# Hybrid encoder trunk on one core: splitting the weights by transfers instead of by VectorE and GpSimd

## The chip, the core and the metric

One of the eight cores of one Trainium2 chip runs the whole program. The metric is the device time of one execution in microseconds. The kernel before took 1604.42 us, the median of three runs (1602.0 to 1606.68).

## The reference

The program computes two residual layers on 512 tokens of width 1024, in float32: a bidirectional Mamba-2 mixer in layer 0, a two-sided Hyena operator in layer 1, and after each of them a SwiGLU channel mixer and a gated input embedding. Cut to what matters:

```python
for i in range(2):
    hn = rms_norm(h, norm_mix[i])
    h = h + (mamba2_mixer if i == 0 else hyena_mixer)(hn, ...)
    h = h + swiglu(rms_norm(h, norm_ffn[i]), w1[i], w3[i], w2[i])   # (silu(h@w1) * (h@w3)) @ w2
    gate = sigmoid(rms_norm(h, norm_ple[i]) @ ple_gate[i])
    h = h + gate * (p[i] @ ple_proj[i])
return rms_norm(h, final_norm)
```

All time goes into products with weights, 1984 weight tiles of 128 x 128 in all.

## The kernel before

Every product of an activation `x` with a weight `w` is made from three TensorE products in a rounded 32-bit format: each operand is split into a high part (the value rounded to that format) and a low part (value minus high part), and `mm3` (lines 292 to 294) adds `w_hi x_hi`, `w_hi x_lo` and `w_lo x_hi` in PSUM. Activations lie as 128 x 512 tiles, so one weight tile costs three matmuls of 512 columns. Only the gate branch of the Mamba stage (`mix_z`, lines 677 to 679) turns the operands round and uses 256 columns.

The host packs the weight tiles in the order of use, eight to a block: `W` has 248 blocks of 128 x 1024 values, 512 KB each. `weight(key)` hands out the next tile; when the first tile of block b is asked for, `emit_block` has been called for all blocks up to b + 2 (`LOOKAHEAD`). `emit_block` (line 268) loads the block into `w_raw` from SyncE's queue, ScalarE rounds it into `w_hi` (line 274), and VectorE writes `w_lo = w_raw - w_hi` (line 275). For every other block of the Mamba input weights and of the Hyena input weights (`pool_lo`) GpSimd does the subtraction instead. `w_raw`, `w_hi` and `w_lo` have three buffers each; the last four blocks keep their parts in a pool of their own with four.

Blocks 2 to 49 are the Mamba input weights, eight groups of six blocks; 142 to 165 the Hyena input weights. The others are the two SwiGLU stages (66 blocks each), the output projections, gates and the projections of `p` (blocks 0 and 1, and 140 and 141).

`load_split` (line 375) does the same splitting for the constant matrices of the Hyena Fourier transforms: CH (filters, during the first SwiGLU), CF and CI (at the Hyena entry), five pieces of up to 512 KB, loaded from ScalarE's queue into the same `w_raw` buffers.

In a group of the Mamba stage, beside the weights: VectorE makes the five-tap convolution (`pre`, line 595), the decay matrices `M` (758, 759), `xw` (708), `y` (771, 780 and others); ScalarE copies PSUM results, among them the two that start the states `ST` (728, 730), and takes exponentials of `FB` (756); SyncE loads `FB` (750, one broadcast row to 128 partitions, four buffers); GpSimd masks `FB` (752), carries states (724) and makes `y` of line 740. TensorE's small products of a group are lines 688 to 719 (transposes, states) and 769 and 775 (outputs). PSUM has four tiles for weight products (`mm_ps`) and four for the rest (`aux_ps`).

Nothing orders the engines by hand: the framework sorts each engine's instructions at build time, roughly as they are written and as operands come ready, and each engine then runs its own list strictly in order. A DMA stands in the list of the engine whose queue issues it, and waits there.

Of the kernel before, what the change touches and what calls it, by code (L numbers as in the profile page):

```python
# [10 lines left out]
F32 = mybir.dt.float32  # L11
F32R = mybir.dt.float32r
AF = mybir.ActivationFunctionType
ALU = mybir.AluOpType

P = 128
T = 512
D = 1024
KD = D // P
# [3 lines left out]
NG = 8  # L23
NC = 4
TPB = 8
# [3 lines left out]
HALVED = 4  # L29
# [49 lines left out]
def hy_cols(q):  # L79
    return [16 + 2 * q, 8 + 2 * q, 17 + 2 * q, 9 + 2 * q, 2 * q, 2 * q + 1]  # L80
# [13 lines left out]
def weight_order():  # L94
    o = order_mk("proj_0", range(KD), range(2))
    for g in range(NG):
        o += order_ssd_in(g)
    o += order_mk("ssd_out", range(KD), range(0, 8))
    o += order_mk("ssd_out", range(KD), range(8, 16), hold=2)
    for i in range(2):  # L100
        for kind, j in ffn_seq():
            o += order_ffn_up(i, j) if kind == "up" else order_ffn_down(i, j)
        o += order_gate(i)
        if i == 0:
            o += order_mk("proj_1", range(KD), range(2))
            for q in range(KD // 2):
                o += order_mk("hy_in", hy_cols(q), range(KD))
            o += order_mk("hy_out", range(KD), range(0, 4))
            o += order_mk("hy_out", range(KD), range(4, 8), hold=2)
    return o  # L110
# [105 lines left out]
def body(ctx, tc, d, out_):  # L216
    nc = tc.nc
    V, A, G, PE = nc.vector, nc.scalar, nc.gpsimd, nc.tensor
# [1 line left out]
    const = ctx.enter_context(tc.tile_pool(name="const", bufs=1))  # L220
    hpool = ctx.enter_context(tc.tile_pool(name="hpool", bufs=1))
    apool = ctx.enter_context(tc.tile_pool(name="apool", bufs=32))
    wpool = ctx.enter_context(tc.tile_pool(name="wpool", bufs=3))
    npool = ctx.enter_context(tc.tile_pool(name="npool", bufs=1))
    dram = ctx.enter_context(tc.tile_pool(name="dram", bufs=1, space=bass.MemoryType.DRAM))
    psum = ctx.enter_context(tc.tile_pool(name="psum", bufs=4, space=bass.MemoryType.PSUM))
# [28 lines left out]

    order = weight_order()
    nblk = (len(order) + TPB - 1) // TPB
    blocks = {}
    kept = {}
    pos = [0]  # L260
    ssd_blocks = range(2, 2 + 6 * NG, 2)
    hy_first = order.index(("hy_in", 0, hy_cols(0)[0])) // TPB
    hy_blocks = range(hy_first + 2, hy_first + 3 * KD, 2)

    def pool_lo(b):
        return b in ssd_blocks or b in hy_blocks

    def emit_block(b):
        raw = wpool.tile([P, TPB, P], F32, tag="raw", name="w_raw", bufs=3)
        nc.sync.dma_start(raw, d["W"][b])  # L270
        pool = kept.get(b, wpool)
        hi = pool.tile([P, TPB, P], F32R, tag="hi", name="w_hi")
        lo = pool.tile([P, TPB, P], F32R, tag="lo", name="w_lo")
        A.copy(hi, raw)  # L274
        (G if pool_lo(b) else V).tensor_sub(lo, raw, hi.bitcast(F32))  # L275
        blocks[b] = (hi, lo)

    def weight(key, n=1):
        t = pos[0]
        assert order[t] == key, (order[t], key)  # L280
        pos[0] += n
        b = t // TPB
        for ahead in range(b, min(b + 1 + LOOKAHEAD, nblk)):
            if ahead not in blocks:
                emit_block(ahead)
        hi, lo = blocks[b]
        i = t % TPB
        return hi[:, i:i + n, :].rearrange("p a b -> p (a b)"), lo[:, i:i + n, :].rearrange("p a b -> p (a b)")
# [84 lines left out]
    def load_split(pool, src, tag):  # L373
        n = src.shape[1]
        hi = pool.tile([P, n], F32R, tag=tag + "h", name=tag + "h", bufs=1)
        lo = pool.tile([P, n], F32R, tag=tag + "l", name=tag + "l", bufs=1)
        for i in range(0, n, TPB * P):
            s = slice(i, min(n, i + TPB * P))
            raw = wpool.tile([P, TPB * P], F32, tag="raw", name="craw", bufs=3)[:, :s.stop - i]
            nc.scalar.dma_start(raw, src[:, s])  # L380
            A.copy(hi[:, s], raw)
            V.tensor_sub(lo[:, s], raw, hi[:, s].bitcast(F32))
        return hi, lo

    def forward_h(C, mv, U, pool):
# [74 lines left out]
    def hyena_filters(pool):  # L460
# [14 lines left out]
        A.copy(w3h, w3)  # L475
        V.tensor_sub(w3l, w3, w3h.bitcast(F32))
        CH = load_split(pool, d["CH"], "CH")
        yield

# [70 lines left out]
    def ssd(next_norm):  # L550
        pool = sctx.enter_context(tc.tile_pool(name="ssd", bufs=1))
        tags = ("pre", ("FB", "FB"), 4, 2)
        rt = npool.tile([P, NC], F32, tag="rt", name="rt", bufs=2)
        A.activation(rt[:, 0:1], eps_t, AF.Sqrt)
        emit_block(0)
        pr = ple_in(pool, 0, tags)
        nm = Norm("nmix0")
        for k in range(KD):
            nc.sync.dma_start(h[k], d["xT"][k])
        emit_block(1)  # L560
        nc.sync.dma_start(par, d["par"])
        o, n = PAR["cw"][0], PAR["cw"][1] + PAR["cb"][1]
# [422 lines left out]
    def hyena(nm, next_norm):  # L985
# [102 lines left out]
        for q in range(4):  # L1088
            project_u(2 * q)
            project_u(2 * q + 1)  # L1090
            project_x0(2 * q)
            if q == 0:
                CF = load_split(pool, d["CF"], "CF")
                CI = load_split(pool, d["CI"], "CI")
                cih, cil = (c.rearrange("p (fch par cs t) -> p fch par cs t", fch=2, par=2, cs=2) for c in CI)
            UH = convolve(q)
            if q:
                back(q - 1, pq.pop(q - 1))
            pq[q] = convolve_rest(*UH)
            project_x0(2 * q + 1)  # L1100
# [36 lines left out]
```

## Time and profile before

| | us |
|---|---|
| median of three runs | 1604.42 |
| profiled execution | 1609.28 |
| its span, first to last instruction | 1607.5 |
| TensorE busy (7698 matmuls) | 1561.5 |
| VectorE busy | 1057.8 |
| ScalarE busy | 673.7 |
| GpSimd busy | 206.8 |

The stages, in us from the start of the span: the projection of `p` and the first norm up to 45, the Mamba groups to 454, its output projection to 520, SwiGLU to 912, gate, projection and norm to 960, Hyena entry to 990, Hyena to 1198, SwiGLU to 1560, the last gate and norm to the end. Busy times of an engine can be set against the length of a stage; an engine that is busy all the time sets the length. The busy time of a TensorE row includes its pipeline, so a matmul of 512 columns that reads 390 ns is followed by the next after 226 ns.

### The profile page before, as it was taken

Reading aid. Unit: us, or ns where it says so; the run is one execution under the profiler, and the core shown is the slowest. Engines: PE = TensorE matmul, PEld = TensorE weight load, DVE = VectorE, ACT = ScalarE, POOL = GpSimd, SP = SyncE. Lnnn points to the kernel's source line nnn. Section 1 sums busy time; section 2 is a strip of 40 time slices with the busy share of each in tenths; the row PEclk is TensorE's granted clock in tenths of the full one; section 3 lists DMA queues with packets and bytes.
Section 4 is the critical chain, followed back from the end, with each engine's and each line's share of the span. In section 5 each row is a group of like instructions: output and inputs, shape, how many; then the busy total and the mean of one; then the engine's idle time right before and its main releaser. Section 6 shows DMA issues by size and latency. Waiting matters only on the chain.

```text
span 1607.5 us, 19878 instructions
## 1 busy us (share of the span) xinstructions
PE 1561.5 (97%) x7698; PEld 1300.9 (81%) x7698; DVE 1057.8 (66%) x1463; ACT 673.7 (42%) x1111; POOL 206.8 (13%) x153
## 2 busy tenths in 40 slices
PE   7999899999999999999999999999999999999998
PEld 5888778877788788888888877888888888888887
DVE  6778787888956686464345578899974434444464
ACT  6574565656434332232233444343253222222355
POOL 1254343443100000000000002232000000000000
PEclk9999999999999999999999999999999999999999
DMA  6343233433143333342332344333132323322332
GB/s 241 110 147 112 92 104 107 131 105 105 62 138 98 105 118 131 108 148 92 95 102 92 100 156 157 105 105 105 53 92 92 104 93 94 103 92 96 120 100 78
DMA packets 56005, 176.52 MB, mean 110 GB/s; under 512 B 5959, under 2 KB 7175, under 8 KB 54760
## 3 DMA queue, kind: packets, MB, share of 16 engines
q1 hardware_dynamic: 46864, 151.17, 29.5%
q10 hardware_dynamic: 9048, 24.10, 4.2%
q8 instruction: 60, 0.98, 0.2%
q14 instruction: 33, 0.27, 0.1%
HBM read 164.63 MB, written 10.62 MB: 109 GB/s over the span
## 4 chain that ended last, share of the span: by engine, by line
PE 76%; DVE 14%; DMA 4%; ACT 3%; issue 2%; POOL 1%; SPq 0%; ACTq 0%; POOLq 0%; DVEq 0%
PE mm_ps L294 22%; PE mm_ps L292 22%; PE mm_ps L293 22%; DMA FB<-FRd 2%; DVE w_lo L275 2%; DVE xw L708 1%; PE aux_ps L292 1%; PE aux_ps L293 1%; DVE pre L595 1%; PE aux_ps L294 1%; DVE M L758 1%; PE mm_ps L677 1%; PE mm_ps L679 1%; PE mm_ps L678 1%; DVE act L321 1%
## 5 line engine op out<-in xcount | busy, mean ns | idle before, releaser
L292 PE MATMUL mm_ps<-act,w_hi 128*128 128x512 f32 (+1 forms) x1856 | 723.3, 390 | 0.0
L293 PE MATMUL mm_ps<-act,w_hi 128*128 128x512 f32 (+1 forms) x1856 | 722.1, 389 | 0.9 <-DVE act L321 0.9
L294 PE MATMUL mm_ps<-act,w_lo 128*128 128x512 f32 (+1 forms) x1856 | 721.4, 389 | 0.2 <-DVE w_lo L275 0.2
L274 ACT CAST w_hi<-w_raw 128x1024 fp32r<-128x1024 f32 x248 | 259.8, 1050 | 598.2 <-PE mm_ps L293 435.5
L292 PEld LDWEIGHTS mm_ps<-act,w_hi 128*128 128x128 f32 x1856 | 349.4, 188 | 75.0 <-issue 5.1
L293 PEld LDWEIGHTS mm_ps<-act,w_hi 128*128 128x128 f32 x1856 | 349.3, 188 | 74.8 <-issue 3.6
L294 PEld LDWEIGHTS mm_ps<-act,w_lo 128*128 128x128 f32 x1856 | 349.3, 188 | 72.1 <-issue 2.7
L275 DVE TENSOR_TENSOR w_lo<-w_raw,w_hi 128x1024 fp32r<-128x1024 f32 x213 | 267.4, 1256 | 130.6 <-ACT w_hi L274 118.5
L275 POOL TENSOR_TENSOR w_lo<-w_raw,w_hi 128x1024 fp32r<-128x1024 f32 x35 | 98.9, 2825 | 726.6 <-ACT w_hi L274 704.9
L867 DVE TENSOR_TENSOR fb<-mm_ps,R 128x512 f32<-128x512 f32 x44 | 30.4, 691 | 128.4 <-PE mm_ps L294 128.4
L595 DVE SCALAR_TENSOR_TENSOR pre<-mm_ps,par,pre 128x511 f32<-128x511 f32 (+1 forms) x128 | 93.1, 739 | 3.3 <-ACT pre L591 3.2
L756 ACT ACTIVATE FB<-FB,bcol 128x128 f32<-128x128 f32 x256 | 79.6, 390 | 28.9 <-POOL FB L752 28.8
L864 DVE TENSOR_TENSOR fa<-mm_ps,R 128x512 f32<-128x512 f32 x44 | 30.3, 689 | 82.5 <-PE mm_ps L294 82.5
L875 DVE TENSOR_TENSOR h<-h,mm_ps 128x512 f32<-128x512 f32 x48 | 32.9, 686 | 72.4 <-PE mm_ps L294 72.4
L677 PE MATMUL mm_ps<-w_hi,act 128*128 128x256 f32 x256 | 72.6, 284 | 0.1
L678 PE MATMUL mm_ps<-w_lo,act 128*128 128x256 f32 x256 | 72.6, 284 | 0.0
L679 PE MATMUL mm_ps<-w_hi,act 128*128 128x256 f32 x256 | 72.4, 283 | 0.0
L752 POOL TENSOR_SCALAR_AFFINE_SELECT FB<-FB 128x512 f32<-128x512 f32 x64 | 54.5, 876 | 65.4 <-DMA FB<-FRd 57.4
L677 PEld LDWEIGHTS mm_ps<-w_hi,act 128*128 128x128 f32 x256 | 49.1, 192 | 0.5 <-issue 0.2
L678 PEld LDWEIGHTS mm_ps<-w_lo,act 128*128 128x128 f32 x256 | 49.1, 192 | 0.3
L679 PEld LDWEIGHTS mm_ps<-w_hi,act 128*128 128x128 f32 x256 | 49.1, 192 | 0.0
L320 ACT CAST act<-fb 128x512 fp32r<-128x512 f32 x44 | 27.4, 622 | 32.0 <-DVE fb L868 32.0
(264 smaller groups left out, 1610.1 us busy)
## 6 DMA issues: line engine op xcount, KB each, us to landing
w_raw<-W SPq DMA_DIRECT2D x248, 512.0 KB, 3.5
FB<-FRd SPq DMA_DIRECT2D x32, 512.0 KB, 5.4
pjd<-ppo ACTq DMA_DIRECT2D x16, 256.0 KB, 3.2
Hd<-Ht ACTq DMA_DIRECT2D x4, 1024.0 KB, 4.0
Ht<-Hd ACTq DMA_DIRECT2D x4, 1024.0 KB, 4.7
pj<-pjd ACTq DMA_DIRECT2D x12, 256.0 KB, 3.8
h<-xT SPq DMA_DIRECT2D x8, 256.0 KB, 5.9
dec<-dec ACTq DMA_DIRECT2D x4, 512.0 KB, 3.5
```

Of the source, the lines that this page charges most:

```text
L274: A.copy(hi, raw)
L275: (G if pool_lo(b) else V).tensor_sub(lo, raw, hi.bitcast(F32))
L292: PE.matmul(ps, whi, xhi, start=start, stop=False)
L293: PE.matmul(ps, whi, xlo, start=False, stop=False)
L294: PE.matmul(ps, wlo, xhi, start=False, stop=stop)
L595: V.scalar_tensor_tensor(pre[:, a:b], ps[:, a + o:b + o], pc("cw", 5 * c + j), pre[:, a:b], ALU.mult, ALU.add)
L677: PE.matmul(o, xhi[:, cs], whi, start=k == 0 and c % 2 == 0, stop=False)
L678: PE.matmul(o, xhi[:, cs], wlo, start=False, stop=False)
L679: PE.matmul(o, xlo[:, cs], whi, start=False, stop=k == KD - 1 and c % 2 == 1)
L752: G.affine_select(FB[:, dr], FB[:, dr], pattern=[[0, NC], [1 - 2 * dr, P]], compare_op=ALU.is_ge, fill=BIG, base=0, channel_multiplier=2 * ...
L756: A.activation(e, e, AF.Exp, bias=bcol[:, c, dr * 32 + hd:dr * 32 + hd + 1])
L875: V.tensor_add(h[m], h[m], ps)
```

## The change

The raw tiles are gone. The high part comes from a transfer that casts on its way from memory, issued by GpSimd (`emit_hi`). ScalarE writes the negative of the high part into the low part's tile, and a second transfer, also issued by GpSimd, adds the weights to it on its way (`accum_op=ALU.add`), which leaves weight minus high part. This holds for all 248 blocks and for the five pieces of the constant matrices. `emit_block(b)` also starts the casting load of block b + 1. High parts have five buffers, low parts four. Line numbers behind this place shift by 0 or 1.

```diff
-    wpool = ctx.enter_context(tc.tile_pool(name="wpool", bufs=3))
+    wpool = ctx.enter_context(tc.tile_pool(name="wpool", bufs=4))
...
-    blocks = {}
+    blocks, his = {}, {}
...
-    def pool_lo(b):
-        return b in ssd_blocks or b in hy_blocks
+
+    def emit_hi(b):
+        hi = kept.get(b, wpool).tile([P, TPB, P], F32R, tag="hi", name="w_hi", bufs=HALVED if b in kept else 5)
+        G.dma_start(hi, d["W"][b])
+        his[b] = hi
 
     def emit_block(b):
-        raw = wpool.tile([P, TPB, P], F32, tag="raw", name="w_raw", bufs=3)
-        nc.sync.dma_start(raw, d["W"][b])
-        pool = kept.get(b, wpool)
-        hi = pool.tile([P, TPB, P], F32R, tag="hi", name="w_hi")
-        lo = pool.tile([P, TPB, P], F32R, tag="lo", name="w_lo")
-        A.copy(hi, raw)
-        (G if pool_lo(b) else V).tensor_sub(lo, raw, hi.bitcast(F32))
+
+        if b not in his:
+            emit_hi(b)
+        hi = his.pop(b)
+        lo = kept.get(b, wpool).tile([P, TPB, P], F32R, tag="lo", name="w_lo", bufs=HALVED if b in kept else 4)
+        A.mul(lo, hi.bitcast(F32), -1.0)
+        G.dma_start(lo, d["W"][b], accum_op=ALU.add)
         blocks[b] = (hi, lo)
+        if 0 < b < nblk - 1:
+            emit_hi(b + 1)
...
-            raw = wpool.tile([P, TPB * P], F32, tag="raw", name="craw", bufs=3)[:, :s.stop - i]
-            nc.scalar.dma_start(raw, src[:, s])
-            A.copy(hi[:, s], raw)
-            V.tensor_sub(lo[:, s], raw, hi[:, s].bitcast(F32))
+            G.dma_start(hi[:, s], src[:, s])
+            A.mul(lo[:, s], hi[:, s].bitcast(F32), -1.0)
+            G.dma_start(lo[:, s], src[:, s], accum_op=ALU.add)
```

The lists of the engines change with it. The first matmuls on TensorE, before (`pp` is the split `p`, block 0 its weights, `S` and `dg` belong to the first norm):

```order
L292 MATMUL mm_ps<-pp,w_hi 128x512 x3
L293 MATMUL mm_ps<-pp,w_hi 128x512
L294 MATMUL mm_ps<-pp,w_lo 128x512
L292 MATMUL mm_ps<-pp,w_hi 128x512
L293 MATMUL mm_ps<-pp,w_hi 128x512
L294 MATMUL mm_ps<-pp,w_lo 128x512
```

And of the changed kernel:

```order
L293 MATMUL mm_ps<-pp,w_hi 128x512
L294 MATMUL mm_ps<-pp,w_hi 128x512
L348 MATMUL aux_ps<-ones,S 128x1 x4
L356 MATMUL aux_ps<-dg,ones 128x512
L295 MATMUL mm_ps<-pp,w_lo 128x512
L293 MATMUL mm_ps<-pp,w_hi 128x512
L294 MATMUL mm_ps<-pp,w_hi 128x512
L295 MATMUL mm_ps<-pp,w_lo 128x512 x2
```

The piece of the changed list begins with the last of four such pairs: eight products with the high part stand first, then both steps of the norm, and the first product with a low part comes after them.

VectorE in a Mamba group, around the `y` of line 771, before:

```order
L275 TENSOR_TENSOR w_lo<-w_raw,w_hi 128x1024
L598 SCALAR_TENSOR_TENSOR sx_1806<-sx_1806,pre 128x512
L799 TENSOR_SCALAR y<-y,rs 128x256 x6
L275 TENSOR_TENSOR w_lo<-w_raw,w_hi 128x1024
L595 SCALAR_TENSOR_TENSOR pre<-mm_ps,par,pre 128x510
L771 TENSOR_TENSOR y<-y,aux_ps 128x512
```

The same place in the changed kernel:

```order
L799 TENSOR_SCALAR y<-y,rs 128x256 x4
L598 SCALAR_TENSOR_TENSOR sx_1782<-sx_1782,pre 128x512
L799 TENSOR_SCALAR y<-y,rs 128x256
L595 SCALAR_TENSOR_TENSOR pre<-mm_ps,par,pre 128x510
L771 TENSOR_TENSOR y<-y,aux_ps 128x512
```

The two weight rows ahead of `y` are gone; the rest of the work keeps its order nearly.

GpSimd in one Mamba group, before:

```order
L740 TENSOR_TENSOR y<-XT,par 128x1024
L275 TENSOR_TENSOR w_lo<-w_raw,w_hi 128x1024
L752 AFFINE_SELECT FB<-FB 128x512 x2
L724 TENSOR_TENSOR stt<-ST,eL 128x256 x4
L752 AFFINE_SELECT FB<-FB 128x512 x2
L275 TENSOR_TENSOR w_lo<-w_raw,w_hi 128x1024
L752 AFFINE_SELECT FB<-FB 128x512 x4
L275 TENSOR_TENSOR w_lo<-w_raw,w_hi 128x1024
```

The first part of such a group in the changed kernel:

```order
L752 AFFINE_SELECT FB<-FB 128x512
L724 TENSOR_TENSOR stt<-ST,eL 128x256 x2
L752 AFFINE_SELECT FB<-FB 128x512
L274 DMA w_lo<-W 128x1024
L724 TENSOR_TENSOR stt<-ST,eL 128x256
L264 DMA w_hi<-W 128x1024
L752 AFFINE_SELECT FB<-FB 128x512 x3
L274 DMA w_lo<-W 128x1024
L264 DMA w_hi<-W 128x1024
L752 AFFINE_SELECT FB<-FB 128x512 x2
L274 DMA w_lo<-W 128x1024
```

Three subtractions of a group have become twelve DMAs, some of them behind masks that wait for `FB`; SyncE's list keeps only `FB` and the first and last transfers.

## Rows read from the trace of the kernel before

**Rows 1.** Busy us (and instructions) per engine in stages, then clock, DMA share, GB/s.
```profile
core 0: us, PE busy (x) PEld busy (x) DVE busy (x) ACT busy (x) POOL busy (x), PEclk, DMA share, GB/s
45.00:454.00 409.00, 388.13 (x2224) 326.91 (x2224) 333.82 (x483) 241.93 (x540) 153.01 (x126) 0.99 0.34 108
990.00:1198.00 208.00, 200.27 (x1026) 170.35 (x1025) 185.72 (x264) 77.69 (x107) 39.40 (x16) 0.99 0.30 97
1198.00:1560.00 362.00, 362.00 (x1600) 299.35 (x1599) 168.06 (x200) 111.86 (x134) 0.00 (x0) 1.00 0.31 100
```
**Rows 2.** TensorE's waits from 45 to 454 us: total us, times, longest.
```profile
PE aux_ps L775 <- DVE y L771: 8.6, 5, 3.3
PE aux_ps L719 <- DVE xw L708: 7.4, 6, 1.9
PE aux_ps L719 <- ACT w_hi L274: 3.6, 4, 1.1
```
**Rows 3.** Timeline in a Mamba group: start, duration, instruction [idle before it].
```profile
167.78 2.49 DVE L275 TENSOR_TENSOR w_lo<-w_raw,w_hi 128x1024 fp32r<-128x1024 f32 x1 [3.65 <-issue]
170.19 0.73 DVE L595 SCALAR_TENSOR_TENSOR pre<-mm_ps,par,pre 128x510 f32<-128x510 f32 x1
...
171.57 1.46 PE L775 MATMUL aux_ps<-ST,sC 128*128 128x512 f32 x2 [3.33 <-DVE y L771]
```
**Rows 4.** TensorE's waits from 945 to 1198 us, and VectorE's weight rows from 960.
```profile
PE aux_ps L1041 <- DVE act L1017: 5.5, 4, 1.9
...
L275 DVE TENSOR_TENSOR w_lo<-w_raw,w_hi 128x1024 fp32r<-128x1024 f32 x23 | 28.0, 1218 | 5.6 <-ACT w_hi L274 5.5
```
**Rows 5.** Groups by line, whole span: busy us, mean ns, idle before and releaser.
```profile
L275 DVE TENSOR_TENSOR w_lo<-w_raw,w_hi 128x1024 fp32r<-128x1024 f32 x213 | 267.4, 1256 | 130.6 <-ACT w_hi L274 118.5
...
L274 ACT CAST w_hi<-w_raw 128x1024 fp32r<-128x1024 f32 x248 | 259.8, 1050 | 598.2 <-PE mm_ps L293 435.5
```
**Rows 6.** Timeline of TensorE at the start.
```profile
10.46 0.63 PE L292 MATMUL mm_ps<-pp,w_hi 128*128 128x512 f32 x1
...
10.89 0.63 PE L293 MATMUL mm_ps<-pp,w_hi 128*128 128x512 f32 x1
...
18.34 1.02 PE L355 MATMUL aux_ps<-dg,ones 128*128 128x512 f32 x2
...
21.96 0.39 PE L294 MATMUL mm_ps<-pp,w_lo 128*128 128x512 f32 x1
...
24.64 0.44 PE L293 MATMUL aux_ps<-act,wd 128*64 128x512 f32 x1 [1.73 <-DVE act L321]
```
**Rows 7.** Transfers: a queue's packets, MB, engine share; issues, KB, us to landing; issue ns.
```profile
q1 hardware_dynamic: 46864, 151.17, 29.5%
...
w_raw<-W SPq DMA_DIRECT2D x248, 512.0 KB, 3.5
...
Hd<-Ht ACTq DMA_DIRECT2D x4, 1024.0 KB, 4.0
...
L270 SPq DMA_DIRECT2D w_raw<-W x248: 327/328/716, 0.7 to 1555.4; - x124
```
**Rows 8.** GpSimd: one kind of wait, and groups by line from 45 to 454 us.
```profile
POOL FB L752 <- DMA FB<-FRd: 57.4, 19, 6.8
...
L275 POOL TENSOR_TENSOR w_lo<-w_raw,w_hi 128x1024 fp32r<-128x1024 f32 x22 | 58.7, 2670 | 96.8 <-ACT w_hi L274 96.8
L752 POOL TENSOR_SCALAR_AFFINE_SELECT FB<-FB 128x512 f32<-128x512 f32 x64 | 54.5, 876 | 65.4 <-DMA FB<-FRd 57.4 <-DVE sx L598 2.8 <-DVE pre L595 2.4
L740 POOL TENSOR_TENSOR y<-XT,par 128x1024 f32<-128x1024 f32 x8 | 19.2, 2404 | 69.9 <-ACT XT L696 69.9
```
**Rows 9.** Chain of work that ended last: the same transposes three Mamba groups apart.
```profile
177.28 0.87 PE aux_ps L695 x8
...
324.29 0.87 PE aux_ps L695 x8
```
**Rows 10.** VectorE, group of line 799 from 45 to 454 us.
```profile
L799 DVE TENSOR_SCALAR y<-y,rs 128x256 f32<-128x256 f32 x32 | 9.3, 357 | 0.1
```

More of the change, by code (lines that the diff above doesn't have):

```diff
@@ L257, in body @@
     nblk = (len(order) + TPB - 1) // TPB
-    blocks = {}
+    blocks, his = {}, {}
     kept = {}
     pos = [0]
-    ssd_blocks = range(2, 2 + 6 * NG, 2)
-    hy_first = order.index(("hy_in", 0, hy_cols(0)[0])) // TPB
-    hy_blocks = range(hy_first + 2, hy_first + 3 * KD, 2)
-    def pool_lo(b):
-        return b in ssd_blocks or b in hy_blocks
-    def emit_block(b):
-        raw = wpool.tile([P, TPB, P], F32, tag="raw", name="w_raw", bufs=3)
-        nc.sync.dma_start(raw, d["W"][b])
-        pool = kept.get(b, wpool)
-        hi = pool.tile([P, TPB, P], F32R, tag="hi", name="w_hi")
-        lo = pool.tile([P, TPB, P], F32R, tag="lo", name="w_lo")
-        A.copy(hi, raw)
-        (G if pool_lo(b) else V).tensor_sub(lo, raw, hi.bitcast(F32))
+    def emit_hi(b):
+        hi = kept.get(b, wpool).tile([P, TPB, P], F32R, tag="hi", name="w_hi", bufs=HALVED if b in kept else 5)
+        G.dma_start(hi, d["W"][b])
+        his[b] = hi
+    def emit_block(b):
+        if b not in his:
[4 more added lines that the diff above has]
+        G.dma_start(lo, d["W"][b], accum_op=ALU.add)
         blocks[b] = (hi, lo)
+        if 0 < b < nblk - 1:
+            emit_hi(b + 1)
     def weight(key, n=1):
```

## The prediction

> **What bounds the kernel now.** I read the busy time of each stage first. In the two SwiGLU stages TensorE is busy for the whole stretch: 362.0 of 362.0 us for 1600 matmuls, 226 ns each, so a block of eight weight tiles (24 matmuls) lasts 5.43 us there [rows 1]. No speed of another engine is worth anything in such a stretch. TensorE stands still in the Mamba stage, 409.0 - 388.1 = 20.9 us, and in the Hyena stage, 208.0 - 200.3 = 7.7 us, and there VectorE is busy 333.8 and 185.7 us, 82% and 89% [rows 1]. Next I read what ended those waits. In the Mamba stage three waits hold 19.6 us: 8.6 for `y` of line 771, 7.4 for `xw` of line 708, 3.6 for ScalarE, which stood at a `w_hi` cast [rows 2]. The timeline shows how the first arises: VectorE runs a `w_lo` subtraction of 2.49 us ahead of `y`, and the matmuls of line 775 wait 3.33 us [rows 3]. In the Hyena stage 5.5 of the 7.7 us wait for line 1017 on VectorE, which spends 28.0 us on `w_lo` there [rows 4]. So the reader should see two things: low parts hurt where VectorE is nearly full, and are free elsewhere.
>
> **What is removed.** VectorE loses 213 subtractions, 267.4 us, GpSimd the other 35; ScalarE's 248 casts of 1050 ns [rows 5] become 248 scalings of the same tile, which I take at the same price (they write as many elements; 0.9 to 1.2 us would change nothing in stages that are not ScalarE's). Of the 267.4 us the SwiGLU stages give nothing back. In the Mamba stage the order on VectorE shows no weight row ahead of line 771 any more, and on ScalarE none between the two copies into `ST`: the 8.6 and 3.6 us can go. What is late next there are the `pre` rows of line 595, 0.73 us each, still queued ahead of `y` [rows 3], about 0.4 us in each of five groups, so I take 12.2 - 2 = 10 us. The 7.4 us for `xw` I leave, since GpSimd's product of line 740 stays (2404 ns, on the same `XT`) [rows 8]. In the Hyena stage I take 6 of 7.7 us. The bounds of this gain are 0 and all that TensorE stands there, 28.6 us.
>
> **What is added at the start.** Block 0's low part now needs a load, a scaling and a second transfer one after another. The order on TensorE answers by putting the norm's matmuls behind eight high-part products; the accumulators allow no more. In the trace the norm's last product starts at 18.34 us, and 35 of the 48 `pp` products were done by then; the last of them starts at 21.96 us [rows 6]. So 27 products are late, 27 x 0.226 = 6.1 us, of which a later pause of 1.7 us in TensorE [rows 6] takes up some: +4.5 us. Ends: 0 if the low part lands before its place matters, and 10 if the late products run 0.43 us apart, as those at 10.46 and 10.89 us do [rows 6].
>
> **What is added everywhere: two transfers per block on GpSimd's queue.** Three prices have no row, since no transfer before was cast, accumulated or issued there. *Issue.* SyncE needs 0.33 us [rows 7]; GpSimd needs 2.4 us for a whole tile of this size [rows 8]. I take 1 us, nearer to the issue. Even the upper end fits: a Mamba group lasts (324.29 - 177.28)/3 = 49.0 us [rows 9], GpSimd's other work in it is (153.0 - 58.7)/8 = 11.8 us [rows 1, 8], and 12 x 2.4 = 28.8 us more make 40.6; in SwiGLU 4.8 of 5.43 us. *Transfer engines.* SyncE's queue moved 151.17 MB in 29.5% of the span, 474 us, so a block's 0.524 MB takes 1.65 us [rows 7]. The casting load I count the same, since it moves the same bytes. The accumulating one also reads its destination back: between 1.65 (the read is hidden) and 4.94 us (read, read back and write one after another). I take two passes, 3.29 us, because one 1.65 already covers a read with its write. A block then asks 4.94 us where SwiGLU gives 5.43: it fits, with 9% to spare, and in the Mamba stage with a third. *Landing.* 3.5 us for a plain load, and 4.0 more for a separate store of twice the size [rows 7] bound the accumulating transfer at 3.5 to 7.5 us; I take 5. The low part is ordered two blocks ahead of its use, 10.9 us in SwiGLU, so 1.05 + 1 + 5 us hide behind 24 matmuls twice over. If that cover is gone, the full difference falls on every block.
>
> A page of the Trainium skill ("Collectives: The Full Stack", section "The bandwidth ceiling: the fold count and why AG ≠ RS ≠ AR") bears on that price: it gives a reduce done in flight about half the rate of a copy, because it reads two sources. By it a block would ask three units of 1.65 us, again 4.94, as an estimate from that page; no row of this trace shows an addition in flight.
>
> **What is moved.** The FB loads stand alone on SyncE now; their masks (line 752) share GpSimd's queue with weight transfers, one or two between masks. The five pieces of CH, CF and CI also go through GpSimd: at the Hyena entry three loads and three additions stand among those of blocks 146 to 150, some 3 x 4.94 = 15 us of transfer work more than five blocks need, against 2 to 3 blocks of lead. I take +2 us, ends 0 and 12.
>
> **Sum.** 1609.3 (profiled execution; its span is 1607.5) - 10 - 6 + 4.5 + 2 = 1599.8. That execution lies 4.9 us above the median of 1604.4, so on the median 1594.9, rounded 1595.
>
> **Rivals.**
> *The transfer engines become the bound.* If the accumulating transfer costs more than 5.43 - 1.65 = 3.78 us, 2.3 passes, TensorE follows the transfers in the 176 blocks that are neither Mamba inputs (48) nor Hyena inputs (24). At 2.5 passes a block asks 5.76 us, +0.33 x 176 = +58, about 1660 us; at three passes 6.58, +1.15 x 176 = +202, about 1800. For it: 9% is little, and queues of two kinds share the engines. Against it: the 29.5% counts packet time, which may hold waiting that overlaps. 24%.
> *GpSimd's queue holds low parts back in the Mamba stage.* A transfer stands behind masks that wait for FB loads: 19 such waits, 57.4 us, the longest 6.8 [rows 8]. The lead is two blocks, 2 x 49.0/6 = 16.3 us; a 6.8 wait, two masks (1.8), issue 1 and scaling 1.05 leave 5.7 for the landing. Above that TensorE waits; at 7.5 it is 1.8 us, twice in each of eight groups, +29, about 1624 us. For it: FB loads will meet twice the traffic. Against it: SyncE no longer keeps them behind weight loads. 13%.
> *VectorE locks GpSimd out.* The only sizeable VectorE rows in the Mamba stage with one tensor and a scalar are 32 of line 799, 9.3 us in all [rows 10]; SwiGLU has none. If each held up a transfer by its own length and TensorE waited for all of it, +9.3 us: 1604. 3%. The rule behind it is in the Trainium skill ("SBUF — State Buffer", section "SBUF: two separate sides"): while a copy or a tensor-with-scalar operation of VectorE uses both of its ports, GpSimd cannot write the descriptors of its transfers. By that page the subtractions of two tensors that go away were not of this kind; no row here shows a transfer of GpSimd's at all.
> *A wash.* VectorE's time comes back, but the start (up to 10), the Hyena entry (up to 12) and later FB loads eat it: 1600 to 1609. 18%. That the change does not do what it says is excluded by the order: no subtraction is left on VectorE.
>
> **How the numbers follow.** The forecast, 1595, has 42%; its own range is 1580 (all but 4 us of the 28.6 gained, nothing paid: 1604.4 - 24.6) to 1599. Faster by over 0.3% (about what a measurement of this kernel tells from no change: below 1599.6) is the forecast alone, 0.42; within it the wash and the lock, 0.18 + 0.03 = 0.21; slower the two others, 0.24 + 0.13 = 0.37. The range runs from 1580 to 1700: it holds the queue's case and the first half of the transfer case (up to 2.6 passes); beyond 1700 stay some 15%, below 1580 some 4%.
>
> **What would show it.** Right: in SwiGLU TensorE busy all the time and 226 ns per matmul; the transfer share near 90% there; waits of line 775 for `y` nearly gone; VectorE's share in the Mamba stage under 75%; the start 4 to 5 us later. Wrong: waits of TensorE for `w_lo` transfers in SwiGLU (the engines bound), or in the Mamba stage behind masks (the queue bound); a landing above 5.7 us; an issue above 2.4 us on GpSimd. The forecast falls if one block's two transfers take longer than 5.43 us.

## The result, and the profile after

The changed kernel takes **1629.4 us** (median of four runs, 1627.4 to 1632.8), the kernel before 1603.65: a ratio of 1.016, 95% interval [1.0137, 1.0184]. It is slower by 26 us; 1595 was forecast. The profiled execution took 1629.5 us, its span is 1627.8.

Windows of the changed kernel, in the columns of [rows 1] (TensorE, its weight loads, VectorE, ScalarE, GpSimd, granted clock, transfer share, GB/s):

```profile
0.00:45.00 45.00, 29.90 (x112) 21.81 (x113) 18.89 (x31) 21.89 (x34) 10.52 (x20) 0.92 0.90 253
45.00:454.00 409.00, 385.62 (x2211) 324.54 (x2211) 279.72 (x454) 246.15 (x545) 155.75 (x205) 0.99 0.73 173
520.00:912.00 392.00, 392.00 (x1791) 325.06 (x1790) 144.98 (x237) 119.56 (x148) 93.64 (x133) 1.00 0.88 197
...
1230.00:1570.00 340.00, 340.00 (x1502) 281.62 (x1501) 83.06 (x121) 99.05 (x120) 87.78 (x125) 1.00 0.91 195
```

In both SwiGLUs TensorE is busy all the time (in the second 226 ns a matmul, as in [rows 1]), with the transfer engines at 88 and 91%: no starvation. VectorE in the Mamba window fell from 333.8 us [rows 1] to 279.7, 68%. Queue and issues (KB, us to landing), beside [rows 7]:

```profile
q0 software_dynamic: 72864, 264.80, 73.7%
...
w_hi<-W POOLq DMA_DIRECT2D x248, 512.0 KB, 5.1
w_lo<-W POOLq DMA_DIRECT2D x248, 512.0 KB, 6.6
FB<-FRd SPq DMA_DIRECT2D x32, 512.0 KB, 7.6
pjd<-ppo ACTq DMA_DIRECT2D x16, 256.0 KB, 4.9
```

GpSimd spends 0.55 us (median) on issuing a casting load and 0.86 on an addition:

```profile
L264 POOL DMA_DIRECT2D w_hi<-W x248: 530/552/1589, 1.3 to 1562.7; - x124
...
L274 POOL DMA_DIRECT2D w_lo<-W x248: 849/855/1208, 10.0 to 1569.5; - x124
```

TensorE's waits over the whole span (total us, times, longest):

```profile
PE aux_ps L356 <- DVE dg L353: 9.5, 3, 5.2
PE mm_ps L293 <- DMA w_hi<-W: 8.8, 1, 8.8
PE aux_ps L719 <- DVE xw L708: 8.2, 8, 1.3
PE mm_ps L295 <- DMA w_lo<-W: 6.1, 2, 3.2
PE aux_ps L583 <- ACT dtT L580: 5.9, 1, 5.9
PE aux_ps L775 <- DVE y L771: 4.5, 4, 2.6
PE aux_ps L348 <- DVE S L339: 3.8, 1, 3.8
```

The wait for `y` is half of the 8.6 of [rows 2] and the one for `w_hi` ahead of line 719 is gone. New are waits at the start (`w_hi`, `S`, `dtT`) and at norms (`dg`).

**Where the time went.** The order of TensorE's work is nearly the same, so the first matmul of a step can be set beside itself in two traces: the transposes of `dtT` (line 583), and the sums of the norms ahead of the first SwiGLU (N2), Hyena (N4), the second SwiGLU (N5) and the last gate (N6). In the kernel before they start at 36.8, 524.1, 954.1, 1196.2 and 1557.2 us. The table gives how much longer (+) or shorter a stage is than there, in us. A second trace of the kernel before, taken with the experiments, differs by at most 0.5 in any stage.

| | start to `dtT` | to N2 (Mamba) | to N4 (SwiGLU, gate) | to N5 (Hyena) | to N6 (SwiGLU) |
|---|---|---|---|---|---|
| changed kernel | +14.8 | -5.2 | -0.7 | +4.2 | +7.2 |
| first 2 blocks old | +2.6 | -5.6 | -0.7 | +2.9 | +6.6 |
| first 8 blocks old | -1.0 | -11.8 | -0.7 | +2.2 | +6.7 |
| first 8, CF, CI, CH old | -1.1 | -4.9 | -0.8 | +0.8 | +7.4 |
| first 8 and all behind Hyena old | -0.8 | -12.6 | -0.7 | +5.5 | -0.1 |
| new in Mamba's groups 1 to 7 alone | +1.9 | -11.3 | -0.7 | +3.1 | -0.1 |
| no addition | +7.4 | -18.9 | -0.7 | -7.3 | 0.0 |
| no addition, dummy of 384 KB | +12.1 | +0.1 | -0.7 | -1.4 | +0.4 |
| no addition, dummy of 512 KB | +13.5 | +10.9 | +1.3 | -1.8 | 0.0 |

The first line adds up to 20.3 us, the difference of the two spans. (By medians it is 26: both traced executions of the kernel before, 1609.3 and 1610.1 us, lie above its median, which matters below.)

These are single executions, and the granted clock of each moves its stages. In both traces of the kernel before, TensorE falls to its lower level (0.50 of the clock, 1.2 instead of 2.4 GHz) three times in Mamba, in the first of them behind waits of 1.95, 3.33 and 1.91 us (twice for `y`, once for `xw`). That costs some 5.1 us there in each trace (an estimate: the busy time of every us, times what its clock lacks to 1), beside the waits themselves. The windows of the first trace:

```profile
120.00:125.00 5.00, 4.14 (x9) 2.64 (x10) 5.00 (x10) 0.00 (x0) 0.00 (x0) 0.66 0.53 197
170.00:175.00 5.00, 3.43 (x8) 2.19 (x9) 5.00 (x10) 0.00 (x0) 0.00 (x0) 0.72 0.62 213
235.00:240.00 5.00, 3.97 (x9) 2.06 (x10) 4.17 (x7) 0.37 (x1) 2.59 (x4) 0.71 0.53 165
```

The line with CF, CI and CH old has three such falls in Mamba as well, again some 5.1 us, and stands at -4.9; the line above it makes all of Mamba's blocks in the same way, has none, and stands at -11.8. So the Mamba column is good to some 7 us, and a difference of 2 or 3 us in the other columns is weak. The timed runs show the clock too: the changed kernel was granted 0.988 or 0.989 of it, the kernel before 0.996 (median of 24 runs). By that at most (0.996 - 0.9885) x 1628 = 12 of the 26 us are TensorE at its lower level, an estimate from above, since the clock while it stands still counts in it.

**The start, in rows.** The first product waits for the casting load until 8.76 us (5.96 before). ScalarE stands 3.95 us at the first scaling, and the squares of the norm stand behind it:

```profile
8.65 1.06 ACT L273 ACTIVATE w_lo<-w_hi 128x1024 fp32r<-128x1024 f32 x1 [3.95 <-DMA w_hi<-W]
9.61 0.61 ACT L335 ACTIVATE S<-h 128x512 f32<-128x512 f32 x1
...
45.95 0.58 ACT L544 COPY ppo<-mm_ps 128x512 f32<-128x512 f32 x1 [6.56 <-DMA pjd<-ppo]
...
50.88 0.58 ACT L580 COPY dtT<-aux_ps 64x512 f32<-64x512 f32 x1 [1.71 <-DMA pjd<-ppo]
```

The products of `pp` come late, so their copies into the two `ppo` tiles stretch to 47 us, among weight transfers that fill the engines. The store issued at 38.00 us is what the copy at 45.95 waits for, and `dtT` stands behind it. TensorE, idle from 45.7 to 51.6 us, is granted 0.50 of its clock next, and loses some 2.6 us more by it (an estimate: 3.40 x 0.50 + 5.00 x 0.18):

```profile
45.00:50.00 5.00, 0.68 (x3) 0.22 (x2) 0.00 (x0) 2.23 (x3) 0.54 (x1) 1.00 0.89 274
50.00:55.00 5.00, 3.40 (x11) 2.73 (x12) 2.44 (x5) 2.42 (x4) 0.31 (x1) 0.50 0.71 111
55.00:60.00 5.00, 5.00 (x20) 4.04 (x19) 2.31 (x4) 2.39 (x3) 0.56 (x1) 0.82 0.08 12
```

**Behind Hyena, in rows** (ScalarE first, then TensorE, then the window):

```profile
1206.27 0.71 ACT L324 ACTIVATE act<-h,par 128x512 fp32r<-128x512 f32 x1
1210.93 1.06 ACT L273 ACTIVATE w_lo<-w_hi 128x1024 fp32r<-128x1024 f32 x1 [3.95 <-DMA w_hi<-W]
1214.61 1.06 ACT L273 ACTIVATE w_lo<-w_hi 128x1024 fp32r<-128x1024 f32 x1 [2.63 <-DMA w_hi<-W]
1215.58 0.25 ACT L350 ACTIVATE rt<-aux_ps,eps_t 128x4 f32<-128x4 f32 x1
```
```profile
1209.26 0.95 PE L348 MATMUL aux_ps<-ones,S 128*128 128x1 f32 x8
...
1216.90 1.19 PE L356 MATMUL aux_ps<-dg,ones 128*128 128x512 f32 x1 [5.23 <-DVE dg L353]
```
```profile
1200.00:1215.00 15.00, 11.68 (x56) 9.49 (x54) 3.89 (x6) 4.88 (x7) 3.37 (x5) 0.96 1.09 276
```

The norm's sums are ready at 1210.2 us, but its root stands on ScalarE behind two scalings whose high parts have not landed, while the engines are full (share 1.09). TensorE runs dry for 5.23 us.

### The profile page after: what moved, and what is told of

The parts are those of the page before. It is cut to its first block, busy times and chain, and to the rows that moved or that the text cites. A ratio compares the mean times of both kernels' runs of the same rounds, so it can differ in the third digit from the quotient of the medians.

```text
span 1627.8 us, 20086 instructions
## 1 busy us (share of the span) xinstructions
PE 1564.4 (96%) x7698; PEld 1303.3 (80%) x7698; DVE 773.2 (48%) x1245; ACT 672.8 (41%) x1111; POOL 454.0 (28%) x624
## 3 DMA queue, kind: packets, MB, share of 16 engines
q0 software_dynamic: 72864, 264.80, 73.7%
## 4 chain that ended last, share of the span: by engine, by line
PE 80%; DMA 7%; issue 4%; DVE 4%; ACT 2%; POOL 2%; SPq 0%; POOLq 0%; ACTq 0%; DVEq 0%
PE mm_ps L295 22%; PE mm_ps L294 22%; PE mm_ps L293 22%; DMA w_hi<-W 2%; DMA FB<-FRd 2%; DMA pjd<-ppo 2%; PE mm_ps L679 1%; PE mm_ps L678 1%; PE mm_ps L677 1%; PE aux_ps L769 1%; PE aux_ps L293 1%; DMA w_lo<-W 1%; PE aux_ps L295 1%; PE aux_ps L294 1%; PE aux_ps L719 1%
## 5 line engine op out<-in xcount | busy, mean ns | idle before, releaser
L273 ACT ACTIVATE w_lo<-w_hi 128x1024 fp32r<-128x1024 f32 x248 | 262.4, 1059 | 639.0 <-PE mm_ps L295 479.9
L264 POOL DMA_DIRECT2D w_hi<-W x248 | 153.5, 623 | 606.0 <-PE mm_ps L295 574.3
L274 POOL DMA_DIRECT2D w_lo<-W x248 | 214.3, 867 | 364.8 <-ACT w_lo L273 334.5
L595 DVE SCALAR_TENSOR_TENSOR pre<-mm_ps,par,pre 128x510 f32<-128x510 f32 (+1 forms) x128 | 94.3, 743 | 67.4 <-ACT pre L591 66.9
L752 POOL TENSOR_SCALAR_AFFINE_SELECT FB<-FB 128x512 f32<-128x512 f32 x64 | 45.9, 766 | 76.1 <-DMA FB<-FRd 73.7
L339 DVE TENSOR_TENSOR S<-S,sq 128x512 f32<-128x512 f32 x42 | 29.0, 691 | 35.4 <-ACT sq L338 34.8
```

The costliest lines, as they stand in the source:

```text
L264: G.dma_start(hi, d["W"][b])
L273: A.mul(lo, hi.bitcast(F32), -1.0)
L274: G.dma_start(lo, d["W"][b], accum_op=ALU.add)
L595: V.scalar_tensor_tensor(pre[:, a:b], ps[:, a + o:b + o], pc("cw", 5 * c + j), pre[:, a:b], ALU.mult, ALU.add)
L752: G.affine_select(FB[:, dr], FB[:, dr], pattern=[[0, NC], [1 - 2 * dr, P]], compare_op=ALU.is_ge, fill=BIG, base=0, channel_multiplier=2 * ...
```

## The experiments

**What the additions cost.** The first edit is in both places, for the weights and for CF, CI and CH:

```
-        G.dma_start(lo, d["W"][b], accum_op=ALU.add)
+        G.dma_start(lo, d["W"][b])
```

> The changed kernel with all its transfers in place, but the second transfer of a block overwrites the low tile instead of adding to it, so it moves the same bytes without the read of the destination (the low parts are then the weights themselves; only the time is looked at). By the page, the GpSimd queue's engine share is 73.7%: at 1.64 us a plain 512 KB that leaves some 3.1 us for an accumulation. Theory A (queueing at the transfer engines makes landings late at start, Hyena's entry and the norms): share falls to about 50%, landings of w_hi from 5.1 to 4 or less, 8 to 15 us gone: 1614 to 1621. Rival B (the length of the chain load, scaling, issue, second load, and ScalarE's order, whatever the engines' load): 1624 to 1630.

Measured 1592.96 us, 0.9935 [0.9918, 0.9951] of the kernel before: 36 us less than the changed kernel, on theory A's side and more than it said.

```profile
q0 software_dynamic: 72864, 264.80, 55.2%
...
w_hi<-W POOLq DMA_DIRECT2D x248, 512.0 KB, 3.9
w_lo<-W POOLq DMA_DIRECT2D x248, 512.0 KB, 4.6
FB<-FRd SPq DMA_DIRECT2D x32, 512.0 KB, 6.9
```

55.2% of 1588.1 us for 264.80 MB is 1.74 us a casting 512 KB; 73.7% of 1627.8 is 323 us more, over 253 additions 1.28 each, so an addition takes 3.0. Both landings are shorter. Load or landing? Two runs add load without an addition:

```
+        G.dma_start(dram.tile([96, TPB, P], F32, tag="dummy", name="dummy", bufs=8), d["W"][b][:96])
```

> The kernel without addition (the low part is overwritten by the weights, so the values differ), with a further transfer of 384 KB from DRAM to DRAM behind each low part on the same queue, nobody waiting for it: about the 1.26 us of engine time by which an accumulation (73.7% of 1627.8 us) was dearer than the same transfer without addition (55.2% of 1588.1 us) over some 256 transfers. Theory A (engine load: the queue at 87% and more cannot catch up where stages begin): 1618 to 1632. Rival L (the accumulation's own later landing, 6.6 against 4.6 us, in the chain of one block): 1591 to 1600.

Measured 1621.38 us, 1.0117 [1.0099, 1.0134]; 28.4 of the 36.4 us are back, for dummies of 0.93 us (68.5% of 1617.6 us, less the 876.6 us of the run without them, over 248).

> The kernel without addition (values differ, as there) with the dummy transfer enlarged from 384 to 512 KB, so that by scale it takes 0.93 x 4/3 = 1.24 us of engine time, an addition's 1.28. Theory A (all of the 36 us are engine load): 1626 to 1634, and from Hyena's norm to the last one 366 us or more, where 361 without load. Rival L (8 us, among them the loss behind Hyena, belong to the addition's own later landing in its block's chain): 1620 to 1625, and 361 us behind Hyena.

Measured 1635.03 us, 1.0205 [1.0184, 1.0225].

```profile
q0 software_dynamic: 80800, 394.84, 71.7%
...
FB<-FRd SPq DMA_DIRECT2D x32, 512.0 KB, 11.0
```

By the first row a dummy took 1.18 us. The totals lie near the changed kernel's, but the dummies did not run where the additions run. They wait for nothing, and all 248 are issued before 968 and 982 us, some 2 us into Hyena at the latest. The issues in the two runs:

```profile
L275 POOL DMA_DIRECT2D dummy<-W x248: 486/501/576, 8.7 to 967.8; - x124
L275 POOL DMA_DIRECT2D dummy<-W x248: 486/501/581, 10.5 to 982.1; - x124
```

Mamba's window without addition, with dummies of 384 KB and with those of 512 KB:

```profile
45.00:454.00 409.00, 400.23 (x2302) 340.14 (x2301) 289.00 (x465) 251.18 (x551) 146.22 (x214) 1.00 0.61 186
45.00:454.00 409.00, 385.04 (x2210) 324.62 (x2209) 283.50 (x448) 244.26 (x543) 186.60 (x307) 0.99 0.83 269
45.00:454.00 409.00, 377.46 (x2156) 317.32 (x2154) 276.36 (x434) 240.76 (x533) 185.86 (x303) 0.98 0.90 296
```

In it 100 and 99 dummies stand beside some 50 blocks, two to a block, at transfer shares of 0.83 and 0.90 where the additions make 0.73. That the totals agree is therefore luck, and neither theory is decided by them or by the stage behind Hyena, in which no dummy ran. What the two runs do show is that load without additions costs Mamba time: by the table 19.0 and 29.8 us more than without addition, for some 1.9 and 2.3 us of load a block (estimates: 100 x 0.93 and 99 x 1.18, over 50). The additions, 1.28 us a block, cost 13.7 us there. All three are 10 to 13 us for each us of load a block, so load can make all of what the additions cost in Mamba, within the 7 us to which that column is good. A dummy's issue also takes GpSimd 0.50 us, but between the two runs only the size differs, and that alone makes 10.8 us; FB lands after 11.0 us with the larger dummies, 6.9 without. Whether the 11.5 us that the additions cost in Hyena and the 7.2 us behind it come from load or from the addition's own later landing stays open: no run separates the two there.

**Where it is paid.** The old way was brought back for a range of blocks, the raw tile in one of the `w_hi` buffers:

```
+        if old(b):
+            raw = wpool.tile([P, TPB, P], F32, tag="hi", name="w_raw", bufs=5)
+            nc.sync.dma_start(raw, d["W"][b])
+            ...
+            A.copy(hi, raw)
+            (G if pool_lo(b) else V).tensor_sub(lo, raw, hi.bitcast(F32))
```

> The changed kernel, but its first eight weight blocks (both pp products and Mamba's group 0) are made in the old way: raw load on SyncE, cast on ScalarE, subtraction on VectorE or GpSimd, the raw tile in one of the five w_hi buffers. Matched product by product, TensorE in the changed kernel is 14 to 16 us behind the kernel before by 52 us and stays so through group 0. Theory A (that loss is made by the new transfers of these eight blocks alone): 1629.4 - 14 = 1612 to 1618, and the shift at the dtT transposes falls from 14.8 to under 3. Rival B (a lead that the changed kernel loses anyway once the accumulating transfers begin, at block 8 instead of block 0): 1624 to 1631, with the shift back at 10 or more by group 1.

`old(b)`: `b < 8`. Measured 1607.89 us, 1.003 [1.0016, 1.0044]: 21.5 us gone, theory A and more.

> The changed kernel with only its first two weight blocks (both for the pp products) made in the old way. With the first eight old, 21.5 us went. Theory F (the late first product and ScalarE's scaling ahead of the squares of the norm, both in blocks 0 and 1, make the start's loss): 1608 to 1615. Rival Q (the transfers of blocks 2 to 7, beside which the stores of the projection land up to 8 us late): 1620 to 1628.

`b < 2`. Measured 1617.1 us, 1.0078 [1.0052, 1.0104]: 12.3 us gone, between the two theories and nearer to F. `dtT` comes 2.6 us late instead of 14.8. The start's loss begins in the first two blocks; the other 9 us go with blocks 2 to 7, Mamba's group 0, whose transfers run beside the stores.

> The changed kernel with its first eight blocks and all blocks behind Hyena's inputs (Hyena's output, second SwiGLU, last gate) made in the old way. Theory A (the norm behind Hyena waits on ScalarE behind scalings whose high parts are late, 6.7 us in the trace of the old start alone): 1607.9 - 7 = 1599 to 1603. Rival B (Hyena's own transfers leave a backlog that the norm meets anyway): 1605 to 1610.

`b < 8 or b >= hy_first + 3 * KD`. Measured 1602.25 us, 1.0009 [0.9984, 1.0034]; the stage behind Hyena is back at -0.1. Theory A, though with a wide interval for the 5.6 us between the two medians, and in its trace Hyena is 3.3 us longer than with the old start alone. No backlog from Hyena shows behind it.

> The changed kernel with its first eight blocks and also CF, CI and CH made in the old way (loads on ScalarE's queue, cast, subtraction on VectorE, raw tiles in the w_hi buffers). Beside the kernel with the old start alone (1607.9): Theory C (the three casting loads and three accumulations of CF and CI on GpSimd's queue make the 8.6 us that are lost from 954 to 985 us of the kernel before): 1599 to 1603. Rival W (the weights' own transfers lose it, between the stores of the second projection and the norm): 1605 to 1610.

```
-            G.dma_start(hi[:, s], src[:, s])
-            A.mul(lo[:, s], hi[:, s].bitcast(F32), -1.0)
-            G.dma_start(lo[:, s], src[:, s], accum_op=ALU.add)
+            nc.scalar.dma_start(raw, src[:, s])
+            A.copy(hi[:, s], raw)
+            V.tensor_sub(lo[:, s], raw, hi[:, s].bitcast(F32))
```

Measured 1607.52 us, 1.003 [1.0014, 1.0046], as with the old start alone: theory C falls. CF, CI and CH cost nothing that the times show.

**Whether ScalarE's place is at fault.**

```
-        A.mul(lo, hi.bitcast(F32), -1.0)
+        G.tensor_scalar_mul(lo, hi.bitcast(F32), -1.0)
```

> The changed kernel with the scaling by -1 on GpSimd instead of ScalarE, everything else the same. Theory S (ScalarE stands in its order at scalings whose high part has not landed, 132 us in 44 waits, and the norms' squares and roots behind it are late): ScalarE's waits for w_hi vanish, TensorE's wait behind the norms (9.5 us for dg, 3.8 for S) mostly too: 1614 to 1622. Rival T (the transfers and the stores behind them are late, not the scaling's place): 1627 to 1635. Rival G (GpSimd, which took 2.57 us for a subtraction of this tile in the kernel before, now holds its own issues back): 1635 to 1680.

Measured 1655.99 us, 1.0312 [1.0277, 1.0347]: rival G.

```profile
L273 POOL TENSOR_SCALAR w_lo<-w_hi 128x1024 fp32r<-128x1024 f32 x248 | 717.3, 2892 | 227.7 <-DMA w_hi<-W 124.0 <-issue 46.5 <-PE mm_ps L295 14.6
```

A scaling takes 2.89 us there, and the issues now stand behind it, and behind the high part's landing. That ScalarE's order is the last link of the two chains above is read from their rows; this run does not isolate it.

**How much lead the buffers give.**

> New transfers for blocks 8 to 49 (Mamba's groups 1 to 7) and Hyena's input blocks only; all other blocks, CF, CI and CH in the old way, raw tiles sharing six w_hi buffers, three w_lo buffers. Theory A (the Mamba and Hyena gains are real, 10 to 12 and 5 us, and the losses belong to start, Hyena's entry and the norm behind Hyena): 1603.7 - 10 - 5 = 1585 to 1592. Rival B (TensorE only won back there what it had lost at the start, waits absorbed by a late start): 1600 to 1606. Rival C (three w_lo buffers hold the scaling back): TensorE waits for w_lo in Mamba, 1606 to 1625.

```
+        return not (8 <= b < 2 + 6 * NG or hy_first + 2 <= b < hy_first + 3 * KD)
```

Measured 1638.77 us, 1.0221 [1.0194, 1.0247]: rival C.

```profile
PE mm_ps L697 <- DMA w_lo<-W: 24.0, 10, 6.0
PE mm_ps L313 <- DMA w_lo<-W: 12.8, 5, 4.2
```

> As the hybrid with three w_lo buffers, but with five w_hi buffers (shared with the raw tiles) and four w_lo buffers, as in the changed kernel: new transfers for blocks 8 to 49 (Mamba's groups 1 to 7) and Hyena's input blocks, all else old, CF, CI and CH too. Theory A (four w_lo buffers keep a block of lead that three took away, and the stages' gains are real): Mamba 10 us and Hyena 6 us gained and nothing lost between: 1603 - 16 = 1584 to 1592. Rival C (the loss in the hybrid was the sharing of the w_hi buffers, not the fourth w_lo buffer): 1615 to 1640.

Measured 1602.62 us, 1.0005 [0.9991, 1.0018]: a fourth `w_lo` buffer, with one `w_hi` buffer fewer, is worth 36 us. So the first hybrid lost its time by three `w_lo` buffers, its rival C, and yet theory A's gain is missing.

```
-  ... name="w_hi", bufs=HALVED if b in kept else 5)      -  ... name="w_lo", bufs=HALVED if b in kept else 4)
+  ... name="w_hi", bufs=HALVED if b in kept else 4)      +  ... name="w_lo", bufs=HALVED if b in kept else 5)
```

> The changed kernel with one buffer moved: five of w_lo, four of w_hi. Theory L (the chain scaling, issue, addition of one block is too long for the lead that the w_lo buffers give; three of them instead of four cost 36 us in the hybrid): a block more of lead takes away most of the losses at Hyena's entry and behind Hyena, 1612 to 1622. Theory A (the engines' queue is full there, a lead that cannot be filled helps nothing): 1625 to 1634. Rival H (four w_hi buffers hold back the casting loads): 1635 or more.

Measured 1923.02 us, 1.1996 [1.1962, 1.203]: rival H, far beyond its size. In SwiGLU, ScalarE in the changed kernel and then here:

```profile
809.41 1.06 ACT L273 ACTIVATE w_lo<-w_hi 128x1024 fp32r<-128x1024 f32 x1 [3.30 <-PE mm_ps L295]
...
814.85 1.06 ACT L273 ACTIVATE w_lo<-w_hi 128x1024 fp32r<-128x1024 f32 x1 [3.86 <-PE mm_ps L295]
```
```profile
801.54 1.06 ACT L273 ACTIVATE w_lo<-w_hi 128x1024 fp32r<-128x1024 f32 x1 [8.36 <-DMA w_hi<-W]
...
810.16 1.06 ACT L273 ACTIVATE w_lo<-w_hi 128x1024 fp32r<-128x1024 f32 x1 [7.56 <-DMA w_hi<-W]
```

In the changed kernel a scaling is released by TensorE, every 5.44 us: the high part has long landed. With four `w_hi` buffers each scaling waits for a landing, and the next high part's issue stands on GpSimd behind the addition that waits for this scaling. Load, scaling and issue then follow one another, and from 700 to 912 us the transfer share is 0.67 while TensorE is busy 184 of 212 us.

**What the gain in Mamba is worth.**

> New transfers for Mamba's groups 1 to 7 alone (blocks 8 to 49, five w_hi and four w_lo buffers); start, SwiGLUs, gates and all of Hyena in the old way. Theory A (the gain of 9 to 13 us that the traces show inside Mamba stands by itself): 1591 to 1597. Rival R (by the times the Mamba gain is not there: the version with Mamba and Hyena gave 1602.6 by its runs although its trace was 8 us ahead of that of before): 1600 to 1605.

`old(b)`: `not 8 <= b < 2 + 6 * NG`. Measured 1603.56 us, 1.0009 [0.9993, 1.0025]: rival R. In its trace TensorE stands still in Mamba's window for 409.0 - 392.9 = 16.1 us, 20.9 in [rows 1], and the clock never falls there:

```profile
45.00:454.00 409.00, 392.93 (x2269) 332.10 (x2268) 294.97 (x470) 247.24 (x543) 143.80 (x188) 1.00 0.68 167
```

So of the 11.3 us in the table some 5 are waits, and some 5 the clock that both traces of the kernel before lose in Mamba. Start and Hyena stand at +1.9 and +3.1 in this trace though nothing is new there; the runs do not show why. The buffers that its old blocks share need not be the reason: the kernel before with more subtractions on GpSimd (below) keeps its own buffers and has +1.9 and +2.4.

> The kernel before, once more, for a second trace: whether its products stand where the first trace had them. Theory A (differences of stages under 3 us between two traces are drift of the run, above all of the granted clock): within 4 us of 1603.7, shifts between the two traces up to 4 us. Rival (the first trace, at 1609.3, was a late one throughout): 1600 to 1603, with the difference in one place.

1610.1 us, and the first trace's stages within 0.5 us. The traced executions of the kernel before are about 7 us above its timed runs (1602.5, the median of 24). Their granted clock is 0.993 and 0.994; 17 of the 24 timed runs have 0.996 or more. So part of what the traces show as gained in Mamba, the clock's part above all, is, by these clocks, time that most of the timed runs never lost.

> The kernel before with one edit: all of Mamba's low parts subtracted on GpSimd, where before every second one was. No transfer changes. Theory V (what the new transfers gain in Mamba is that VectorE no longer subtracts, 1.22 us for every second block): as much gained here, 1592 to 1598. Rival G (GpSimd at 2.57 us a subtraction, 15.4 us of a group's 49 beside the masks, is late with masks or low parts): 1604 to 1620.

`ssd_blocks = range(2, 2 + 6 * NG)` in the kernel before. Measured 1605.37 us, 1.0012 [0.9998, 1.0027]: in rival G's range, not in theory V's. Taking every subtraction off VectorE there gains nothing.

> New transfers only for every second block of Mamba's groups 1 to 7 and of Hyena's inputs, those whose subtraction stood on VectorE; GpSimd subtracts the others as in the kernel before, and all else is old. VectorE is relieved as with all blocks new, at half the additions. Theory A (the additions' load on the transfer engines takes back part of the gain even there): 1594 to 1600, below the 1602.6 of the version with all these blocks new. Rival B (VectorE's relief is worth no more than what the runs showed, nothing measurable): 1600 to 1604. Rival G (GpSimd, with a subtraction of 2.57 us between its issues, holds loads back): 1605 to 1620.

`old(b)`: `not ((8 <= b < 2 + 6 * NG and b % 2) or (hy_first + 2 <= b < hy_first + 3 * KD and (b - hy_first) % 2))`. Measured 1624.62 us, 1.0141 [1.0118, 1.0163].

> The same for Mamba's groups 1 to 7 alone, Hyena old. Theory A: 1596 to 1601, below the 1603.6 of the version with all of Mamba's blocks new. Rival B: 1601 to 1605. Rival G: 1605 to 1620.

`old(b)`: `not (8 <= b < 2 + 6 * NG and b % 2)`. Measured 1624.11 us, 1.0133 [1.0118, 1.0148]: on rival G's side in both, and some 4 us beyond its range. In the second trace:

```profile
PE aux_ps L794 <- DVE y L790: 11.9, 7, 3.0
```

The wait for `y` is longer than in [rows 2], 11.9 instead of 8.6 us. That GpSimd, with subtractions and issues on one queue, is what is late is argued and not shown: VectorE waits only 1.2 us for GpSimd's masks there. No version here that makes the low parts is measurably faster than the kernel before; the best, with the old way at both ends, equals it.

## Why the prediction was wrong

- *Bounds and prices: right.* SwiGLU gave nothing and starved nowhere. The issue (0.55 and 0.86 us) was below the 1 us taken, the casting load (1.74) near 1.65, the addition (3.0) below 3.29, so 4.74 of 5.43 us a block where 4.94 was reckoned. The page "Collectives: The Full Stack" of the Trainium skill, section "The bandwidth ceiling: the fold count and why AG ≠ RS ≠ AR", gives a reduce half a copy's rate; here it is 1.74/3.0 = 0.58 of it.
- *Where it failed: "it fits, with 9% to spare".* The sum took load on the engines as free as long as a block's transfers fit into a block's time, and so had no term for what the additions do to other work. That holds in mid-SwiGLU, where TensorE never waits at shares of 0.88 and 0.91. Elsewhere the additions cost 36 us: without them the kernel takes 1592.96 us, close to the 1595 that were forecast. In Mamba the dummies show that load does this without any addition, although the transfers fit: 2 x 1.74 + 2.3 = 5.8 us a block, where a block has 49.0/6 = 8.2 [rows 9], and still 29.8 us more.
- *The start: +4.5, ends 0 and 10.* Measured +14.8 in the trace, 21.5 by time for the first eight blocks. The sum counted late products. It left out that ScalarE stands at a scaling ahead of the norm's squares, that the stores of `ppo` land late and `dtT` waits behind them, and that TensorE is granted half its clock after these waits.
- *Mamba: -10.* -5.2 in the changed kernel, -11.8 with the old start, -18.9 without additions. VectorE at 68% and the halved wait for `y` are as foretold. But TensorE's idle time in Mamba fell by only some 5 us in the version with this gain alone; the rest of its -11.3 is the clock. And the term was taken from the profiled execution, then subtracted from the median: the timed runs of that version show no net gain (1.0009). Whether those 5 us are hidden there by losses in other stages, no run shows. That execution's excess over the median should have warned that what it lost is not all in the median.
- *Hyena: -6 + 2.* Measured +4.2. Without additions it is -7.3, so the gain was sized well and the additions, 11.5 us, eat it, by load or by landing. The +2 was put on the wrong cause, CF and CI.
- *Behind Hyena: no term.* Measured +7.2. The text said that the low part hides behind 24 matmuls twice over, and did not ask what stands behind a scaling in ScalarE's order when it does not.
- *Landing: 5 us, bound 5.7 for Mamba.* Measured 6.6. By the second rival TensorE should then wait in Mamba for low parts, about 1624. Its two waits for `w_lo`, 6.1 us in all, cannot make 26: that time was near, its mechanism was not this. The first rival (SwiGLU starved) did not come about. The rule on VectorE's ports (the page "SBUF — State Buffer", section "SBUF: two separate sides") shows in no row: the longest issue of an addition took 1.21 us, the median 0.86; the longest of a casting load, 1.59 us at 164.85 us, ran beside lines 595 and 598 of VectorE, not beside line 799.
- *The range*, 1580 to 1700, held the time, by luck: its upper part came from two rivals whose mechanisms did not come about. A slower kernel had been given 0.37.

## What to carry to other kernels

Moving arithmetic into transfers trades a busy engine for load on a shared queue. Price that load at stage boundaries, where something waits for a store or a first tile, and not only against the steady rate. When a dummy load stands in for another, compare where it ran before comparing the totals. Look at what stands behind each new wait in the order of the engine that does the waiting, here a norm's root behind a scaling. And before a gain is subtracted from a median, ask whether the profiled execution is a typical one.

## What the runs showed of the hardware

- An accumulating 512 KB transfer takes 3.0 us of the 16 engines, a casting one 1.74, a plain one 1.64 (from [rows 7]). Transfers for which nobody waits, 1.9 and 2.3 us of them a block, made Mamba 19.0 and 29.8 us longer.
- GpSimd scales a 128x1024 tile in 2.89 us, more than the 2.67 of a subtraction of two such tiles [rows 8]; ScalarE takes 1.06.
- One tile buffer more or less was worth 36 us (`w_lo`) and some 300 (`w_hi`), with the same transfers. With one `w_hi` buffer fewer, the next load's issue stood behind an addition whose scaling waited for the last landing.
